# One pass over the gated outputs in the first output projection: both column halves of a chunk together

## The chip, the core and the metric

The kernel runs on one core of a Trainium2 chip. The metric is the device time of one execution in microseconds (us). The kernel before took 2925.76 us (median of 3 runs, 2924.88 to 2928.11). A profiled execution of its own took 2932.84 us, of which 2931.1 us lie between the first and the last instruction.

## The reference

The program is one inference step of a decoder with two layers, for a prompt of 2048 positions (width 1024) and a sample group of 8 sequences with 4 positions each. Layer A is gated linear attention with 4 heads of value width 512, layer B is sliding-window attention. Between them lies the part that matters here: layer A's gated output, 2048 wide, goes through an output projection and is added to the residual; the RMS-normalised sum then feeds the shared keys and values and layer B.

```python
o = rmsnorm(o, out_norm_g).reshape(bsz, seq_len, BRANCH_WIDTH)   # 2048 wide
d = (o * jax.nn.silu(gate)) @ w_out                               # 2048 x 1024
hp, hs = hp + dp, hs + ds
k_p, v_p = shared_kv(hp, kv_norm, w_k, w_v, k_norm, pos_p)        # normalises hp
q_p, g_p = swa_query(hp, b_norm[j], b_w_in[j], b_q_norm[j], pos_p)
```

The sample group has a recurrent state for each head and sequence (128 x 512 floats), which is read, used, updated and written back.

## The kernel before

The prompt is cut into 16 chunks of 128 positions and 4 blocks of four chunks. Every product is done in fp16 with operands split in a high and a low half, three matmuls for each product (`PASSES`), so a projection of one chunk on 512 output columns with 2048 inputs is 16 x 3 = 48 matmuls of 128x512.

Layer A runs over 4 heads and 4 blocks. For each chunk, `spill_og` (L613) writes the split gated output to a DRAM tensor, `ogd`. The output projection then reads it back transposed.

The **first output projection** (L1044 to L1050 and L1430 to L1435) goes over the chunks twice: a first pass makes columns 0 to 511 of all 16 chunks, a second pass columns 512 to 1023. `out_steps` (L981) of one chunk and half issues four transposing DMAs of 256 KB from `ogd` (`load`, L997) into four tiles (of the tags `sg` and `v` by turns, four buffers each), then the 48 matmuls into an accumulator `pj` (two buffers), then `a_finish` (L1015): load the input rows (`X`), add (VectorE, L1021), store to `hd`. In the second pass `a_finish` also loads the first half back from `hd` (`E`, L1025), and `norm_T` (L294) normalises the row, splits it and issues two more transposing DMAs (L315) that put it, transposed, into `uT`, the input of layer B.

Four SBUF tags matter. `W` has 12 slots of 4 KB for split weights; a unit of weights is 256 rows by 512 columns, so one half of the output weights takes 8 slots. `uT` has 4 slots of 16 KB; each holds the normalised inputs of one block, first of layer A, later of layer B. `wraw` (3 buffers) takes raw weights from DRAM, and `pst` (2 buffers) split weights on their way back to DRAM.

A **preparation step** (`prepare`, L236) is: load half a unit of raw weights of layer B (256 KB, SyncE queue, L219), round it on ScalarE (L193), take the remainder on VectorE (L194), both into a `pst` buffer, and store that to DRAM (256 KB, issued by GpSimd, L244). There are 104 such steps, and 8 small table steps. They are handed out by `some` between other work; layer B later fetches the prepared weights (`fetch`, L250, 512 KB).

The order of the work is that of program text as the framework's list scheduler rearranges it, fixed when the program is built: each engine and the SyncE queue work through their own list in order. An instruction at the head of a list that waits holds up all that is behind it on that engine. From layer B on (`pin`) the matmuls keep the order of the text.

The sample part of layer A (`SampleA.steps`, L674) has one step per sequence, `seq` (L762): it takes the state from a `W` slot (two sequences share one load of 512 KB), splits it, multiplies, updates it in place (L776) and stores it. For the last head these steps run beside the first output projection.

Of the kernel before, what the change touches and what calls it, by code (L numbers as in the profile page):

```python
# [9 lines left out]
F32 = mybir.dt.float32  # L10
# [9 lines left out]
P = 128  # L20
D = 1024
# [51 lines left out]
def _body(tc, nc, cp, sb, ps, dr, i, o):  # L73
# [67 lines left out]
    rtd = dr.tile([P, NCH, 4, HD], F32, tag="rtd", name="rtd")  # L141
    ogd = [dr.tile([P, 2, BW], F16, tag=f"ogd{c}", name=f"ogd{c}") for c in range(NCH)]
    ogd2 = [dr.tile([P, 2, BW], F16, tag=f"oge{c}", name=f"oge{c}") for c in range(NCH)]
    hd = [dr.tile([P, D], F32, tag=f"hd{c}", name=f"hd{c}") for c in range(NCH)]


# [144 lines left out]

        return [lambda part=todo[x : x + per]: step(part) for x in range(0, len(todo), per)], box

    def norm_T(xh, n, dst, both=False):  # L294
# [12 lines left out]
        for half in range(2):  # L307
            cs = slice(half * 512, half * 512 + 512)
            if both is None:
                pool.tensor_scalar(xh[half], xh[half], r[:n, 0:1], None, ALU.mult)  # L310
                split((xt[0][:n, cs], xt[1][:n, cs]), xh[half], eng=pool)
            else:
                split((xt[0][:n, cs], xt[1][:n, cs]), xh[half], r[:n, 0:1])
        for hl in range(2):
            nc.sync.dma_start(dst(hl), xt[hl][:n], transpose=True)  # L315

    uT = [T("uT", [P, KT, 2, 512], F16, 4) for _ in range(NBL)]
    uTs = C("uTs", [P, KT, 2, SMP], F16)
# [336 lines left out]
    class SampleA:  # L655
# [18 lines left out]
        def steps(self):  # L674
# [85 lines left out]
                mm(bx["po"], bx["Sh"], vst, start=True, stop=False)  # L760

            def seq(b):  # L762
                if b % 2 == 0:
                    bx["sr"] = T("W", [P, 2, 512], F32, NW)
                    nc.sync.dma_start(bx["sr"], i["state_gla"][0, b : b + 2, h].rearrange("b p v -> p b v"))
                sr = bx["sr"][:, b % 2]
                sh = T("pst", [P, 2, 512], F16, 2)
                split((sh[:, 0], sh[:, 1]), sr, SST)
                for n, (a, z) in enumerate(PASSES):
                    mm(bx["po"], bx["qm"][:, a, b, :], sh[:, z], start=False, stop=b == NS - 1 and n == 2)  # L770
                km = T("skn", [96, P], F16, 2)
# [5 lines left out]
                if b % 2:  # L777
# [91 lines left out]
    wo = out_w(i["a_w_out"][0], 0, gs_o)  # L869
# [6 lines left out]
    for n, (h, j) in enumerate(blocks):  # L876
# [23 lines left out]
        if last:  # L900
            ch = [cur.chunk_steps(c) for c in range(3)]
            weave([f for c in range(1, 4) for f in cur.vg_steps(c, (0,))], ch[0] + lv[:3] + ch[1][:3] + lv[3:5] + ch[2][:3])
            run(hw[h + 1].v.steps() if h + 1 < AH else wo.steps()[:8])
# [4 lines left out]
            run(hw[h + 1].g.steps() if h + 1 < AH else wo.steps()[8:])  # L908
        else:
            for c in range(3):  # L910
                more = side[c * 2 : c * 2 + 2] if n < 2 else some(PR[j])
# [69 lines left out]
    def out_steps(wo, half, ogs, finish, c):  # L981
        ot = []

        def load():
            if ogs is ogd2:
                t = T("uT", [P, 4, 8, P], F16, 4)
            elif half == 0 and c == 0:
                tt = [T("W", [P, 2, 8, P], F16, NW) for _ in range(2)]
                t = None
            for q in range(4):  # L990
                if ogs is ogd2:
                    ot.append(t[:, q])
                elif half == 0 and c == 0:
                    ot.append(tt[q // 2][:, q % 2])
                else:
                    ot.append(T(("sg", "v")[c % 2], [P, 8, P], F16, 4))
# [3 lines left out]
        return [load] + st + [lambda: finish(half, c, box[0])]  # L1000

    def out_sample(wo, half, finish_s):
        st, total = sproj_steps(wo.cols(4), 16, lambda: ogTs[0])
# [8 lines left out]

        return st + [fin]

    def a_finish(half, c, pp):  # L1015
        cs = slice(half * 512, half * 512 + 512)
        rows = slice(c * P, (c + 1) * P)
        xr = T("X", [P, 512], F32, 2)
        nc.sync.dma_start(xr, i["x_prompt"][0, rows, cs])
        h = T("st", [P, 512], F32, 2)  # L1020
        dve.scalar_tensor_tensor(h, pp, OSC, xr, ALU.mult, ALU.add)  # L1021
        nc.sync.dma_start(hd[c][:, cs], h)
        if half == 1:
            h0 = T("E", [P, 512], F32, 2)
            nc.sync.dma_start(h0, hd[c][:, :512])  # L1025
            cc = c % 4
            if cc == 0:
                uT[c // 4] = T("uT", [P, KT, 2, 512], F16, 4)
            u = uT[c // 4]
            norm_T((h0, h), P, lambda hl: u[:, :, hl, cc * P : (cc + 1) * P])  # L1030

    def a_finish_s(half, pt):
        cs = slice(half * 512, half * 512 + 512)
        xr = T("X", [SMP, 512], F32, 2)
# [6 lines left out]
            nc.sync.dma_start(h0, hsd[:, :512])  # L1041
            norm_T((h0, h), SMP, lambda hl: uTs[:, :, hl, :])

    weave(prev_tail, [f for c in range(7) for f in out_steps(wo, 0, ogd, a_finish, c)])  # L1044
    wo1 = out_w(i["a_w_out"][0], 1, gs_o)
    for c in range(7, NCH):
        weave(out_steps(wo, 0, ogd, a_finish, c), some() if c > 3 else [])
        if c == 12:
            run(out_sample(wo, 0, a_finish_s))
            run(wo1.steps())  # L1050


    def rope_mul(eng, t1, t2, src, ct, st):
# [373 lines left out]
            return [norm, square, norm_k, norm_q, split_q, norm_2, norm_3, cache, cache_2] + [lambda tq=tq, f=f: f(tq) for tq in range(2) for f in (att, att_2, att_3)]  # L1427


    for c in range(NCH):  # L1430
        weave(out_steps(wo1, 1, ogd, a_finish, c), some())
        if c == 8:
            run(gw[0].steps())
        if c == 10:
            run(out_sample(wo1, 1, a_finish_s))  # L1435

    pin[0] = True
    ORDER = "AffffffffBfAfffffffAfffAfBffff"
# [155 lines left out]
```

## Time and profile before

| | before |
|---|---|
| median of 3 runs | 2925.76 us |
| profiled execution | 2932.84 us |
| its span | 2931.1 us |
| TensorE (PE) busy | 2782.9 us, 95% |
| VectorE (DVE) busy | 1661.4 us, 57% |
| ScalarE (ACT) busy | 1387.7 us, 47% |
| GpSimd (POOL) busy | 1012.3 us, 35% |
| mean granted TensorE clock | 0.988 |

TensorE is the busy engine, so the questions are where it idles and who ends that idle time. The first output projection lies between 1154 and 1559 us of the span: first pass from 1154.2 to 1336.8, second pass from 1336.8 to 1559.2. Times in the views below are counted from the start of the span. "DMA share" is the mean busy share of the 16 DMA engines; it can go a little over 1, since packets overlap.

### The profile page before, as it was taken

The page shows a single profiled execution, that of the slowest core. Times are in us where ns is not written, and L with a number is a line of the kernel's source. Part 1 is how long each engine was busy: PE and PEld are TensorE (multiplying, and loading weights), DVE is VectorE, ACT ScalarE, POOL GpSimd, SP SyncE. Part 2 cuts the span into 40 slices and gives each one's busy share as a digit, 9 for nine tenths or more (in the row PEclk, how much of TensorE's full clock was granted, in tenths as well). Part 3 has the DMA queues.
Part 4 walks back from the last instruction along what each step waited for, and adds up shares of the span by engine and source line. Part 5 has one row for each costly group of instructions (what it writes and reads, how often), then busy time and mean ns, then how long its engine had stood idle before and what let it go on. Part 6 is the DMA issues. An engine that isn't in the chain of part 4 may idle for free.

```text
span 2931.1 us, 51443 instructions
## 1 busy us (share of the span) xinstructions
PE 2782.9 (95%) x19198; PEld 1400.0 (48%) x19198; DVE 1661.4 (57%) x3543; ACT 1387.7 (47%) x3289; POOL 1012.3 (35%) x1407
## 2 busy tenths in 40 slices
PE   6899999999999999999879999999999999999999
PEld 4445444544454444443334555555555555544444
DVE  6776777677767764222223666677767767730000
ACT  6655655465556554212232555566666566630000
POOL 2241233222212311001114676566566557520000
PEclk9999999999999999999999999999999999999999
DMA  8351243124212516999997566867857777799874
GB/s 216 78 131 37 83 133 114 35 90 157 85 55 90 187 37 149 193 237 252 241 227 185 106 127 122 200 111 129 176 112 132 154 145 139 146 225 173 176 148 98
DMA packets 881940, 412.75 MB, mean 141 GB/s; under 512 B 755344, under 2 KB 808536, under 8 KB 881656
## 3 DMA queue, kind: packets, MB, share of 16 engines
q1 hardware_dynamic: 870648, 380.02, 59.7%
q0 software_dynamic: 8960, 29.37, 2.7%
q8 instruction: 150, 2.46, 0.4%
q14 instruction: 102, 0.84, 0.1%
q10 hardware_dynamic: 2080, 0.07, 0.0%
HBM read 136.81 MB, written 99.16 MB: 81 GB/s over the span
## 4 chain that ended last, share of the span: by engine, by line
PE 56%; DMA 11%; DVE 10%; ACT 9%; issue 6%; POOL 5%; SPq 3%; ACTq 0%; DVEq 0%; POOLq 0%
PE pj L99 42%; PE tr L99 5%; PE o L99 4%; PE kv L99 3%; ACT o L1198 2%; DMA pre<-pst 2%; DMA pst<-v 2%; DVE v L194 1%; ACT v L193 1%; PE lev L99 1%; SPq L315 1%; DVE o L1193 1%; DMA wraw<-in_a_w_in_dram 1%; DMA uT<-ogT 1%; POOL ogT L191 1%
## 5 line engine op out<-in xcount | busy, mean ns | idle before, releaser
L99 PE MATMUL pj<-W,uT 128*128 128x512 f16 x6528 | 1514.1, 381 | 9.3 <-DVE sg L471 3.4
L99 PEld LDWEIGHTS <-uT 128*128 128x128 f16 x8064 | 775.2, 98 | 874.0 <-issue 40.0
L99 PE MATMUL tr<-W,uT 128*128 128x512 f16 x1536 | 365.7, 379 | 0.0
L1198 ACT ACTIVATE o<-o,mx 128x256 f32<-128x256 f32 (+1 forms) x384 | 168.6, 439 | 185.5 <-DVE mx L1193 175.9
L182 POOL TENSOR_SCALAR rs_m<-ss 128x1 f32<-128x1 f32 (+3 forms) x190 | 44.9, 236 | 607.0 <-ACT og L604 244.7
L99 PEld LDWEIGHTS <-X 128*128 128x128 f16 x2496 | 160.2, 98 | 123.1 <-issue 22.1
L191 POOL TENSOR_TENSOR ogT<-og,ogT 128x512 f16<-128x512 f32 x132 | 161.3, 1222 | 163.0 <-ACT ogT L190 158.6
L99 PE MATMUL pj<-uT,W 128*128 128x512 f16 (+1 forms) x912 | 186.8, 355 | 25.9 <-DMA uT<-ogT 22.6
L1193 DVE CUSTOM_DVE_ANT_0 o<-o,madd,nsink 128x256 f32<-128x256 f32 (+1 forms) x384 | 184.0, 479 | 44.6 <-PE o L99 39.6
L194 DVE SCALAR_TENSOR_TENSOR v<-o,v 128x512 f16<-128x512 f32 (+1 forms) x192 | 129.0, 672 | 117.5 <-ACT v L193 98.3
L99 PEld LDWEIGHTS <-W 128*128 128x128 f16 x2688 | 138.1, 98 | 118.6 <-issue 17.9
L99 PE MATMUL pj<-W,v 128*128 128x512 f16 x768 | 177.8, 388 | 16.8 <-DMA v<-ogd 16.7
L183 POOL TENSOR_TENSOR rs_r<-rs_m,mhalf 128x1 f32<-128x1 f32 (+2 forms) x186 | 185.4, 997 | 14.7
L244 POOL DMA_DIRECT2D pre<-pst x104 | 72.8, 701 | 338.1 <-DVE pst L194 326.7
L99 PE MATMUL pj<-W,sg 128*128 128x512 f16 x720 | 167.5, 389 | 16.5 <-DMA sg<-ogd 13.4
L1444 DVE SCALAR_TENSOR_TENSOR st<-pj,E 128x512 f32<-128x512 f32 x32 | 22.1, 692 | 269.7 <-PE pj L99 269.5
L501 POOL TENSOR_TENSOR E<-bt 128x256 f32<-128x256 f32 x96 | 73.7, 768 | 191.1 <-DVE X L191 111.4
L99 PEld LDWEIGHTS <-v 128*128 128x128 f16 x768 | 74.5, 100 | 115.5 <-DMA v<-ogd 26.3
L99 PE MATMUL o<-gl,X 128*128 128x256 f16 (+1 forms) x768 | 114.7, 273 | 10.6 <-DMA X<-qe 5.6
L642 ACT ACTIVATE ssg<-pj 128x64 f32<-128x64 f32 (+1 forms) x16 | 3.6, 242 | 253.2 <-PE pj L99 247.8
L99 PEld LDWEIGHTS <-sg 128*128 128x128 f16 x720 | 69.9, 100 | 110.5 <-DMA sg<-ogd 25.3
L99 PEld LDWEIGHTS <-sth 128*128 128x128 f16 x1984 | 100.9, 98 | 39.2 <-DMA sth<-v 10.5
(331 smaller groups left out, 4269.4 us busy)
## 6 DMA issues: line engine op xcount, KB each, us to landing
pre<-pst POOLq DMA_DIRECT2D x104, 256.0 KB, 4.0
W<-pre SPq DMA_DIRECT2D x52, 512.0 KB
ogd<-ogT SPq DMA_DIRECT2D x68, 256.0 KB
wraw<-in_a_w_in_dram SPq DMA_DIRECT2D x64, 256.0 KB
wraw<-in_b_w_in_dram SPq DMA_DIRECT2D x64, 256.0 KB
oge<-ogT SPq DMA_DIRECT2D x64, 256.0 KB
E<-hd SPq DMA_DIRECT2D x48, 256.0 KB
W<-in_state_gla_dram SPq DMA_DIRECT2D x16, 512.0 KB
```

Source lines behind the costliest of these rows:

```text
L99: return order(nc.tensor.matmul(*a, **k))
L182: pool.tensor_scalar(m[:n, :k], ss, a, b, ALU.mult, ALU.add)
L183: pool.tensor_tensor(r[:n, :k], m[:n, :k], mhalf[:n, :k], ALU.pow)
L191: eng.tensor_tensor(lo, src, hi, ALU.subtract)
L193: act(hi, src, AF.Copy, scale=sc)
L194: dve.scalar_tensor_tensor(lo, src, sc, hi, ALU.mult, ALU.subtract)
L244: nc.gpsimd.dma_start(self.pre[:, :, half * 512 : half * 512 + 512], t)
L315: nc.sync.dma_start(dst(hl), xt[hl][:n], transpose=True)
L501: pool.tensor_tensor(Ev[:, :, 0, :], ref, btv[:, :, 0, :], ALU.subtract)
L1193: dve.tensor_tensor_reduce(pm[:, z], pm[:, z], madd.rearrange("p a b -> p (a b)")[:, (2 - nk) * P :], -0.125, nsink[:, g * GRP + h : g * G ...
L1198: act(pm[:, z], pm[:, z], AF.Exp, scale=-1.0, bias=nm_[:, h : h + 1], accum_out=bx["sum"][:, h : h + 1])
L1444: dve.scalar_tensor_tensor(y, pp, OSC, hr, ALU.mult, ALU.add)
```

## The change

- Both halves of a chunk are made one after the other from one set of four transposed tiles (`a_out`). The gated outputs are read once: 64 transposing DMAs of 256 KB fewer.
- The first half of the sum stays in SBUF (tag `E`) until the second is there, so the 16 loads from `hd` go.
- Both halves of the weights must lie in SBUF at once: 16 units, 8 of the first half and 4 of the second in the 12 `W` slots, the other 4 in a `uT` slot whose inputs layer A has finished with (`wo_aside`). Another such slot takes the first chunk's transposed outputs. The second half's raw weights are now loaded in the last two blocks of layer A; in the last but one, 12 such loads with their conversions (8 of the second half, 4 of the first) stand where 6 preparation steps stood.
- Since two `uT` slots are taken, the last block's normalised inputs (chunks 12 to 15) go untransposed to DRAM (`ud`) and are brought back with 8 transposing DMAs at the end.
- The sample states of the last head no longer use `W` slots: each sequence has a load and a store of 256 KB of its own, in two buffers of tag `bt`.
- The preparation steps beside the projection are handed out five per chunk from chunk 4 on, where two stood per chunk and pass from chunk 7 of the first pass on.
- Layer B's first weights (`gw[0]`) are fetched where `W` slots come free: 8 units between the first and the second halves of chunks 14 and 15, 4 behind them, among the transposes from `ud`.

```diff
             def seq(b):
-                if b % 2 == 0:
-                    bx["sr"] = T("W", [P, 2, 512], F32, NW)
-                    nc.sync.dma_start(bx["sr"], i["state_gla"][0, b : b + 2, h].rearrange("b p v -> p b v"))
-                sr = bx["sr"][:, b % 2]
+                if h == AH - 1:
+                    sr = T("bt", [P, 512], F32, 2)
+                    nc.sync.dma_start(sr, i["state_gla"][0, b, h])
...
+    def wo_aside():
+        box_o["first"] = T("uT", [P, 4, 8, P], F16, 4)
+        t = T("uT", [P, 4, 2, 1024], F16, 4)
+        for u in range(4):
+            wo1.units[u].t = t[:, u]
...
+                if n == len(blocks) - 2:
+                    if c == 0:
+                        wo_aside()
+                    more = (wo1.steps()[:8] + wo.steps()[:4])[c * 4 : c * 4 + 4]
...
+    def a_out(c):
+        ot, hs = [], []
+        def load():
+            for q in range(4):
+                ot.append(box_o["first"][:, q] if c == 0 else T(("sg", "v")[c % 2], [P, 8, P], F16, 4))
+                nc.sync.dma_start(ot[q], ogd[c][:, q % 2, q // 2 * D : q // 2 * D + D], transpose=True)
+        def fin(half, pp):
+            xr = T("X", [P, 512], F32, 2)
+            nc.sync.dma_start(xr, i["x_prompt"][0, c * P : (c + 1) * P, cs])
+            h = T(("E", "st")[half], [P, 512], F32, 2)
+            dve.scalar_tensor_tensor(h, pp, OSC, xr, ALU.mult, ALU.add)
+            nc.sync.dma_start(hd[c][:, cs], h)
+            hs.append(h)
+            if half == 0:
+                return
+            if c >= NCH - 4:
+                norm_T(hs, P, lambda hl: ud[cc][:, hl], flat=True)
+                return
...
-    weave(prev_tail, [f for c in range(7) for f in out_steps(wo, 0, ogd, a_finish, c)])
-    wo1 = out_w(i["a_w_out"][0], 1, gs_o)
-    for c in range(7, NCH):
-        weave(out_steps(wo, 0, ogd, a_finish, c), some() if c > 3 else [])
+    for c in range(lead):
+        todo += [aout[c + 1][0]] + aout[c][1][0] + aout[c][1][1]
+    weave(prev_tail, todo)
+    for c in range(lead, tail):
+        aout[c + 1][0]()
+        weave(aout[c][1][0] + aout[c][1][1], some(5))
...
-    for c in range(NCH):
-        weave(out_steps(wo1, 1, ogd, a_finish, c), some())
-        if c == 8:
-            run(gw[0].steps())
+    aout[NCH - 1][0]()
+    weave(aout[tail][1][0] + aout[tail + 1][1][0], some(99))
+    run(gw[0].kv[0].steps() + gw[0].q.steps())
+    weave(aout[tail][1][1] + aout[tail + 1][1][1], [])
+    run(gw[0].g.steps())
+    uT[NBL - 1] = T("uT", [P, KT, 2, 512], F16, 4)
+    for c in range(4):
+        for hl in range(2):
+            nc.sync.dma_start(uT[NBL - 1][:, :, hl, c * P : (c + 1) * P], ud[c][:, hl], transpose=True)
```

Two places of the fixed order, as built. The first is VectorE in the changed kernel, from the end of chunk 4's first half (`E<-pj,X`) to the end of chunk 5's first half; `pst<-wraw` is VectorE's part of a preparation step, `ogT` that of the normalisation.

```order
L1031 SCALAR_TENSOR_TENSOR E_13545<-pj_13482,X_13543 128x512
L195 SCALAR_TENSOR_TENSOR pst_13671<-wraw_13672,gsb,pst_13671 128x512
L195 SCALAR_TENSOR_TENSOR pst_13697<-wraw_13698,gsb,pst_13697 128x512
L195 SCALAR_TENSOR_TENSOR pst_13725<-wraw_13726,gsb,pst_13725 128x512
L195 SCALAR_TENSOR_TENSOR pst_13751<-wraw_13752,gsb,pst_13751 128x512
L195 SCALAR_TENSOR_TENSOR pst_13795<-wraw_13796,gsb,pst_13795 128x512
L1031 SCALAR_TENSOR_TENSOR st_13611<-pj_13548,X_13609 128x512
L195 SCALAR_TENSOR_TENSOR pst_13834<-wraw_13835,gsb,pst_13834 128x512
```

The same engine in the kernel before, in the second pass, from the end of one chunk's half (`st<-pj,X`) past the next.

```order
L1021 SCALAR_TENSOR_TENSOR st_14861<-pj_14804,X_14859 128x512
L304 TENSOR_TENSOR ss_14867<-ss_14867 128x1
L194 SCALAR_TENSOR_TENSOR ogT_14876<-E_14864,rs_r_14872,ogT_14875 128x512
L194 SCALAR_TENSOR_TENSOR ogT_14876<-st_14861,rs_r_14872,ogT_14875 128x512
L194 SCALAR_TENSOR_TENSOR pst_14697<-wraw_14698,pst_14697 128x512
L194 SCALAR_TENSOR_TENSOR pst_14736<-wraw_14737,pst_14736 128x512
L1021 SCALAR_TENSOR_TENSOR st_14954<-pj_14897,X_14952 128x512
```

Between two finished halves there were two preparation steps; in the changed kernel there are 5, then 4, 4, 3, 5, 3, 5, 6, 4, 4 and 1 up to the end of chunk 9, so 43 stand between the end of chunk 4's first half and that of chunk 9's.

The second place is the SyncE queue where the last head's states go through, in the changed kernel, from the first state's store on (`bt`; `sg<-ogd` are the transposed outputs of chunk 4).

```order
L786 DMA out_st_s_dram<-bt_13085 128x512
L769 DMA bt_13164<-in_state_gla_dram 128x512
L786 DMA out_st_s_dram<-bt_13124 128x512
L769 DMA bt_13200<-in_state_gla_dram 128x512
L1032 DMA hd_135<-E_13161 128x512
L1029 DMA X_13367<-in_x_prompt_dram 128x512
L786 DMA out_st_s_dram<-bt_13164 128x512
L1024 DMA_TRANSPOSE sg_13280<-ogd_101 128x8x128
L769 DMA bt_13239<-in_state_gla_dram 128x512
L1024 DMA_TRANSPOSE sg_13282<-ogd_101 128x8x128
```

And in the kernel before, where the four loads of that head's states stand together.

```order
L616 DMA ogd_112<-ogT_12761 256x1x512
L765 DMA W_12988<-in_state_gla_dram 128x2x512
L765 DMA W_13061<-in_state_gla_dram 128x2x512
L765 DMA W_13138<-in_state_gla_dram 128x2x512
L765 DMA W_13205<-in_state_gla_dram 128x2x512
L1022 DMA hd_129<-st_12721 128x512
```

A load of the third state and of each later one now stands in the queue behind the store of the state whose buffer it takes.

## Rows read from the trace of the kernel before

**Rows 1.** The page: busy time by engine, and PE in 40 slices.
```profile
PE 2782.9 (95%) x19198; PEld 1400.0 (48%) x19198; DVE 1661.4 (57%) x3543; ACT 1387.7 (47%) x3289; POOL 1012.3 (35%) x1407
...
PE   6899999999999999999879999999999999999999
```
**Rows 2.** Stages: length, busy us (count) by engine, clock, DMA share, GB/s.
```profile
1000.00:1030.00 30.00, 25.04 (x163) 11.87 (x162) 28.12 (x50) 19.75 (x36) 13.80 (x19) 1.00 0.64 205
...
1154.20:1336.80 182.60, 180.57 (x950) 81.76 (x949) 47.46 (x95) 37.98 (x67) 12.51 (x20) 1.00 1.00 217
1336.80:1559.20 222.40, 186.90 (x902) 79.16 (x900) 58.23 (x100) 62.99 (x129) 34.89 (x63) 0.94 1.09 243
1559.20:1600.00 40.80, 39.53 (x188) 17.85 (x187) 11.77 (x25) 10.93 (x28) 21.28 (x30) 1.00 0.67 189
```
**Rows 3.** PE in order of time: start, length, operation, count, idle before.
```profile
1336.69 10.52 PE L99 MATMUL pj<-W,sg 128*128 128x512 f16 x48
1347.05 10.52 PE L99 MATMUL pj<-W,v 128*128 128x512 f16 x48
...
1359.71 5.35 PE L99 MATMUL pj<-W,sg 128*128 128x512 f16 x24 [1.71 <-DMA sg<-ogd]
```
**Rows 4.** What PE waited for, 1080 to 1620 us: total, times, longest.
```profile
PE pj L99 <- DMA v<-ogd: 16.7, 17, 2.7
PE pj L99 <- DMA sg<-ogd: 13.4, 13, 2.5
...
PE pj L99 <- DVE st L1021: 3.1, 1, 3.1
```
**Rows 5.** SyncE's queue in order of time, second pass.
```profile
1356.45 0.88 SPq L219 DMA_DIRECT2D wraw<-in_b_w_out_dram  x2
1357.42 1.23 SPq L997 DMA_TRANSPOSE sg<-ogd  x1
1358.75 0.53 SPq L1022 DMA_DIRECT2D hd<-st  x1
1359.37 2.59 SPq L997 DMA_TRANSPOSE sg<-ogd  x1
```
**Rows 6.** DMA packets, 1336.8 to 1559.2 us.
```profile
DMA packets 107372, 54.00 MB, mean 243 GB/s; under 512 B 94812, under 2 KB 94812, under 8 KB 107359
```
**Rows 7.** Stores of preparation steps (L244), 980 to 1024 us: starts, landing.
```profile
L244 POOL DMA_DIRECT2D pre<-pst x15: 678/684/730, 982.2 to 1022.8; - x15
...
DMA to landing us min/median/max: 3.0/3.5/4.1
```
**Rows 8.** The same stores, 1236 to 1272 us.
```profile
L244 POOL DMA_DIRECT2D pre<-pst x11: 688/690/690, 1236.5 to 1271.0; - x11
...
DMA to landing us min/median/max: 3.6/5.5/6.1
```
**Rows 9.** The same stores, 1336.8 to 1559.2 us.
```profile
DMA to landing us min/median/max: 3.3/4.8/6.5
```
**Rows 10.** Groups, 1154 to 1337 us: busy, mean ns, idle before and releaser.
```profile
L194 DVE SCALAR_TENSOR_TENSOR pst<-wraw,gsb,pst 128x512 f16<-128x512 f32 x11 | 8.2, 749 | 26.9 <-ACT pst L193 26.9
L193 ACT ACTIVATE pst<-wraw,gsb 128x512 f16<-128x512 f32 x11 | 7.8, 718 | 29.0 <-DMA pre<-pst 29.0
...
L99 PE MATMUL pj<-ogTs,W 128*128 128x64 f16 (+1 forms) x128 | 3.6, 183 | 0.0
```
**Rows 11.** PE and VectorE at one state step in order of time.
```profile
1195.32 0.39 PE L99 MATMUL kv<-ke,skn 96*128 96x512 f16 x1
...
1200.72 0.38 PE L99 MATMUL kv<-ke,skn 96*128 96x512 f16 x1
```
**Rows 12.** VectorE there.
```profile
1201.14 0.69 DVE L776 SCALAR_TENSOR_TENSOR W<-kv,W 128x512 f32<-128x512 f32 x1 [1.13 <-PE kv L99]
```
**Rows 13.** Chain of waits: a raw-weight load from issue to its reader.
```profile
1112.64 2.81 DMA wraw<-in_a_w_out_dram
...
1356.45 4.79 DMA wraw<-in_b_w_out_dram
```

More of the change, by code (lines that the diff above doesn't have):

```diff
@@ L143, in _body @@
     ogd2 = [dr.tile([P, 2, BW], F16, tag=f"oge{c}", name=f"oge{c}") for c in range(NCH)]
+    ud = [dr.tile([P, 2, D], F16, tag=f"ud{c}", name=f"ud{c}") for c in range(NCH - 4, NCH)]
     hd = [dr.tile([P, D], F32, tag=f"hd{c}", name=f"hd{c}") for c in range(NCH)]
@@ L314, in norm_T @@
         for hl in range(2):
-            nc.sync.dma_start(dst(hl), xt[hl][:n], transpose=True)
+            if flat:
+                nc.sync.dma_start(dst(hl), xt[hl][:n])
+            else:
+                nc.sync.dma_start(dst(hl), xt[hl][:n], transpose=True)
     uT = [T("uT", [P, KT, 2, 512], F16, 4) for _ in range(NBL)]
@@ L762, in seq @@
             def seq(b):
-                if b % 2 == 0:
-                    bx["sr"] = T("W", [P, 2, 512], F32, NW)
-                    nc.sync.dma_start(bx["sr"], i["state_gla"][0, b : b + 2, h].rearrange("b p v -> p b v"))
-                sr = bx["sr"][:, b % 2]
+                if h == AH - 1:
+                    sr = T("bt", [P, 512], F32, 2)
+                    nc.sync.dma_start(sr, i["state_gla"][0, b, h])
+                else:
+                    if b % 2 == 0:
+                        bx["sr"] = T("W", [P, 2, 512], F32, NW)
+                        nc.sync.dma_start(bx["sr"], i["state_gla"][0, b : b + 2, h].rearrange("b p v -> p b v"))
+                    sr = bx["sr"][:, b % 2]
                 sh = T("pst", [P, 2, 512], F16, 2)
@@ L868, in _body @@
     run(hw[0].g.steps())
-    wo = out_w(i["a_w_out"][0], 0, gs_o)
+    wo, wo1 = (out_w(i["a_w_out"][0], half, gs_o) for half in range(2))
+    box_o = {}
+    def wo_aside():
[3 more added lines that the diff above has]
+            wo1.units[u].t = t[:, u]
     blocks = [(h, j) for h in range(AH) for j in range(NBL)]
@@ L902, in _body @@
             weave([f for c in range(1, 4) for f in cur.vg_steps(c, (0,))], ch[0] + lv[:3] + ch[1][:3] + lv[3:5] + ch[2][:3])
-            run(hw[h + 1].v.steps() if h + 1 < AH else wo.steps()[:8])
+            run(hw[h + 1].v.steps() if h + 1 < AH else wo.steps()[4:])
             for c in range(1, 4):
@@ L907, in _body @@
                 f()
-            run(hw[h + 1].g.steps() if h + 1 < AH else wo.steps()[8:])
+            run(hw[h + 1].g.steps() if h + 1 < AH else wo1.steps()[8:])
         else:
             for c in range(3):
-                more = side[c * 2 : c * 2 + 2] if n < 2 else some(PR[j])
+                if n == len(blocks) - 2:
+                    if c == 0:
+                        wo_aside()
+                    more = (wo1.steps()[:8] + wo.steps()[:4])[c * 4 : c * 4 + 4]
+                else:
+                    more = side[c * 2 : c * 2 + 2] if n < 2 else some(PR[j])
                 weave(cur.vg_steps(c + 1, (0, 1) if n else (1,)), mix(cur.chunk_steps(c) + lv[(0,3,6)[c]:(3,6,8)[c]], sparts[(0,3,7)[c]:(3,7,99)[c]]) + more)
@@ L984, in load @@
         def load():
[L985 to L989, printed above, removed]
-            for q in range(4):
[L991 to L996, printed above, removed]
+            t = T("uT", [P, 4, 8, P], F16, 4)
+            for q in range(4):
+                ot.append(t[:, q])
                 nc.sync.dma_start(ot[q], ogs[c][:, q % 2, q // 2 * D : q // 2 * D + D], transpose=True)
@@ L1000, in out_steps @@
         return [load] + st + [lambda: finish(half, c, box[0])]
+    def a_out(c):
[5 more added lines that the diff above has]
+        def fin(half, pp):
+            cs = slice(half * 512, half * 512 + 512)
+            xr = T("X", [P, 512], F32, 2)
[6 more added lines that the diff above has]
+                return
+            cc = c % 4
+            if c >= NCH - 4:
+                norm_T(hs, P, lambda hl: ud[cc][:, hl], flat=True)
+                return
+            if cc == 0:
+                uT[c // 4] = T("uT", [P, KT, 2, 512], F16, 4)
+            u = uT[c // 4]
+            norm_T(hs, P, lambda hl: u[:, :, hl, cc * P : (cc + 1) * P])
+        out = []
+        for half, w in enumerate((wo, wo1)):
+            st, box = proj_steps(lambda: PT("pj", [P, 512], bufs=2), lambda k, a: ot[k // 8 * 2 + a][:, k % 8, :], w, 16)
+            out.append(st + [lambda half=half, box=box: fin(half, box[0])])
+        return load, out
     def out_sample(wo, half, finish_s):
@@ L1013, in out_sample @@
         return st + [fin]
[L1015 to L1030, printed above, removed]
     def a_finish_s(half, pt):
@@ L1042, in a_finish_s @@
             norm_T((h0, h), SMP, lambda hl: uTs[:, :, hl, :])
-    weave(prev_tail, [f for c in range(7) for f in out_steps(wo, 0, ogd, a_finish, c)])
-    wo1 = out_w(i["a_w_out"][0], 1, gs_o)
-    for c in range(7, NCH):
-        weave(out_steps(wo, 0, ogd, a_finish, c), some() if c > 3 else [])
-        if c == 12:
-            run(out_sample(wo, 0, a_finish_s))
-            run(wo1.steps())
+    aout = [a_out(c) for c in range(NCH)]
+    tail = NCH - 2
+    lead = 4
+    aout[0][0]()
+    todo = []
+    for c in range(lead):
[4 more added lines that the diff above has]
+        weave(aout[c][1][0] + aout[c][1][1], some(5))
+        if c == 7:
+            for half, w in enumerate((wo, wo1)):
+                run(out_sample(w, half, a_finish_s))
     def rope_mul(eng, t1, t2, src, ct, st):
```

8 lines of the change are left out of this document (4 added, 4 removed).

## The prediction

> **What bounds the kernel now.** The page comes first: TensorE is busy for 95% of the span, and of the 40 slices only two in the middle (1392 to 1539 us) show 8 and 7 tenths; the first two belong to the start [rows 1]. So something is to be had where the projection's second pass runs, or nowhere much. The view by stages gives the size: in the first pass TensorE works 180.57 of 182.6 us, in the second 186.90 of 222.4 us, with a mean granted clock of 0.94, and the DMA share is 1.00 and 1.09 [rows 2]. Next the order in time on TensorE: two halves of 48 matmuls that nothing holds up start 1336.69 and 1347.05 us, 10.36 us apart; after the second, the next half begins in pieces, each behind a transposing DMA [rows 3]. The waits say the same for the stage: 16.7 and 13.4 us for transposed outputs, 3.1 us for VectorE [rows 4]. Each of these waits is short, but there are 30 of them.
>
> Why the transposes are late: they stand in SyncE's queue, which never rests there, and a transposing DMA costs the queue 1.23 us when it finds room and 2.59 us when it does not, against 0.4 to 0.5 us for a plain one [rows 5]. The 16 DMA engines are full. In the second pass 94,812 of 107,372 packets are short ones, and these belong to 96 transposes (4 of `ogd` and 2 of `uT` for each chunk), about 990 each [rows 6]. A transpose moves 256 KB, so the 96 move 25 of the 54.0 MB. Where plain DMAs dominate, a share of 0.64 carries 205 GB/s, 320 GB/s at a full share [rows 2]; the other 29 MB are then 90 us of all engines, and of 1.09 x 222.4 = 242 us the transposes take 152: 1.6 us each, where a plain 256 KB takes 0.8. That is why half the transposes matter.
>
> What the second pass would take if nothing held it up: 16 x 10.36 = 165.8 us, and 3.6 us for the sample's small matmuls [rows 3, 10]. It takes 222.4. **53 us are lost** there, slow clock included, and 2 us in the first pass: 55 us.
>
> **The change part by part.** *Second pass merged into the first.* A chunk now has 20.7 us of matmuls, and besides preparation the DMA engines get 6 transposes and 4 plain 256 KB for it (two `X`, two `hd`): 9.6 + 3.3 = 12.9 us. Before, the second pass asked for 9.6 + 5 x 0.8 and two stores of preparation, 15 us, in 10.36 us. The four transposes of the next chunk have a chunk, 20.7 us, to land, where they had a half. So the waits for `v<-ogd` and `sg<-ogd` go, and the loads of `E<-hd` with them. Removed: 55 us, if nothing else is late. Three things are.
>
> *Preparation steps.* In the built order 43 of them stand on VectorE between the end of chunk 4's first half and the end of chunk 9's. TensorE's work in that stretch is 10 halves, 103.6 us, and the sample's two small products (2 x 3.6 us and their transposes, together 8 us): 112 us. The accumulator has two buffers, so TensorE may run one half, 10.4 us, ahead of VectorE. If a step takes p, TensorE waits 43 x p - 122 us in all. What is p? A step needs one of two `pst` buffers and keeps it for ScalarE's 0.72, VectorE's 0.75 us [rows 10] and the store's landing. At a landing of 5.5 us two buffers give (1.45 + 5.5) / 2 = 3.5 us; measured are 10 intervals in 34.5 us, 3.45 us, with ScalarE waiting 29.0 us for `pre<-pst` [rows 8, 10]. In layer A, with a landing of 3.5 us, 14 intervals take 40.6 us: 2.90 us [rows 7]. These are the two ends. The DMA share was 0.64 around the one [rows 2] and about 1 at the other (the first pass has 1.00). In the changed kernel 8.8 steps a chunk at p = 3.3 us are 29 us, in which DMAs ask for 12.9 + 8.8 x 1.6 = 27 us, a share of 0.93; that is nearer to the second, and I take p = 3.3: **20 us** of waiting (3 at 2.90, 26 at 3.45). It shows as TensorE waiting for VectorE's L1031, not for a DMA.
>
> The Trainium skill (DMA: Bandwidth & Descriptors, section "Anatomy of one DMA") fits such a DMA as 2.0 us plus bytes over 436 GB/s, an estimate of 2.6 us for these 256 KB. By it p would be 2.0 us and the term nothing. The trace disagrees: the shortest landing is 3.0 us, the median in the second pass 4.8 us [rows 7, 9].
>
> *States of the last head.* A sequence's `kv` matmul comes every 5.4 us [rows 11]. State b+2 now needs the buffer of state b: from `kv` to `kv` of two later, VectorE 0.69 us [rows 12], a store, its landing, a load, its landing, then the split of about 1.4 us. A 256 KB load took 2.81 us from issue to reader in a quiet stretch, 4.79 us in a full one [rows 13], and a 256 KB store lands in 3.5 to 5.5 us [rows 7, 8]. With 3.5 us for each the ring takes 0.7 + 7 + 1.4 + two issues at 0.5, near 10 us, against 10.8 us of TensorE's work; but SyncE's queue stands still while it waits for the store, and transposes at 1.2 to 2.6 us stand between [rows 5]. Three turns of the ring, each late by 0 to 5 us: 0 to 15 us, I take **5**. The price is bounded, not read, since no ring of this kind runs before.
>
> *Weights.* In the last but one block 12 conversions replace 6 steps, 4.5 us more on a VectorE that is busy 28.12 of 30 us where TensorE already idles 5 us [rows 2]. It may cost 0 to 5 us or nothing beyond the idle time; I take **2**. The late second-half weights are needed only 15 us into chunk 0, which hides them.
>
> *The end.* Eight fetches go out while chunk 15's first half frees the slots, 20.7 us before they are read; the last four in the last 5 us, and the gate weights are read 10.4 us into layer B. Layer B starts with an idle time of 1.3 us now [rows 2]. The 8 added transposes are 13 us of DMA time at a place with a share of 0.67. I take **1** (between -1 and 4). The two `ud` stores a chunk replace two transposes and are cheaper; with room on the DMA engines there, nothing.
>
> The sum: 55 - 20 - 5 - 2 - 1 = 27 us less. The profiled execution, 2932.84 us, would be 2906; the median shown lies 7.1 us below that execution, and from 2925.8 us the same step gives **2899 us**.
>
> **The rivals.** *Full recovery* (chance 0.20): the steps run at layer A's 2.90 us and the ring is hidden. Then 3 + 1 of the 55 us stay, 2875 us. For it: only the packets that are gone make DMA room; against it, the share of 0.93 that the steps themselves bring. The fit of the Trainium skill named above would lead here too; the rows speak against its 2.6 us.
>
> *The wait changes hands* (0.14): steps at 3.45 us and a ring late by 15 us: 26 + 15 us, and 5 for weights and end: 46 us return, 2917 us, and up to no change where the landing reaches the 6.5 us that was seen once in the second pass [rows 9]: p = 4.0, 50 us.
>
> *Slower* (0.08): the same chain of preparation, beyond that point. All 43 steps sit in front of finished halves on VectorE, so a landing of 7.0 us, p = 4.2, costs 59 us, and with the other 8 us the time is 2938 us. It decides from a landing of 6.7 us on. For it: the order crowds 8.8 steps into a chunk, where two in 10.36 us already came with landings of 5.5 us. Against it: a stalled TensorE issues fewer transposes, which shortens the landing.
>
> *That the change does not do what it says* is not open: the built order has 64 transposes of `ogd` instead of 128.
>
> **How the numbers follow.** Forecast 0.58 (2884 to 2913 us), full recovery 0.20 (2866 to 2884), the wait changes hands 0.14 (2913 to 2932), slower 0.08. A measurement can tell 0.2%, about 6 us, from no change. The range from 2870 to 2921 us holds the forecast, most of full recovery and a part of the third case. Faster by more than 0.2% (below 2920): 0.58 + 0.20 + 0.06 = 0.84; within: 0.08; slower: 0.08.
>
> **What would show it.** Right: in the stage TensorE's waits for `v<-ogd` and `sg<-ogd` are below 5 us together; a wait for VectorE's L1031 stands first, between chunks 4 and 9; chunks 10 to 15 run at 20.7 us each with a DMA share well under 1; stores of preparation come every 3.2 to 3.4 us; the clock stays near 1. Wrong: TensorE still waits for transposes, or waits at `o<-pst` in the state steps for more than 15 us, or layer B begins with more than 5 us of waiting for `W<-pre`.

## The result, and the profile after

The changed kernel takes **2900.35 us** (median of 4 runs, 2895.21 to 2904.33) against 2926.94 us for the kernel before on the same chip (4 runs, 2924.88 to 2938.87). The ratio, taken from the mean times, is 0.99, with a 95% interval from 0.9869 to 0.9931: faster by 0.7 to 1.3%. The forecast was 2899 us.

The profiled execution has a span of 2898.0 us, 33.1 us less than that of before. The page after, in the lines of [rows 1] (busy time of the engines, TensorE in 40 slices) and two lines more: the granted clock in tenths, and the packets of the whole span.
```profile
PE 2769.2 (96%) x19198; PEld 1401.8 (48%) x19198; DVE 1661.5 (57%) x3543; ACT 1386.7 (48%) x3289; POOL 1012.0 (35%) x1407
...
PE   6899999999999999997999999999899999999999
...
PEclk9999999999999999998999999999999999999999
...
DMA packets 813331, 393.86 MB, mean 136 GB/s; under 512 B 687760, under 2 KB 740952, under 8 KB 813048
```
The two weak slices of the second pass have become one, at 1304 to 1377 us. The matmuls are as many as before (19,198). Of the packets under 512 B 67,584 are gone (755,344 before), 1056 for each of the 64 transposes that the change drops, near the 990 worked out from [rows 6].

What such a transpose costs can be read from the page's line on the DMAs that SyncE issues (packets, MB, share of the 16 engines' span), before and after:
```profile
q1 hardware_dynamic: 870648, 380.02, 59.7%
q1 hardware_dynamic: 802040, 361.14, 56.3%
```
59.7% of 2931.1 us less 56.3% of 2898.0 us are 118 us of all engines. The 18.9 MB that went are the 64 transposes and, net, 8 plain DMAs of 256 KB (16 reloads fewer, 8 stores to `ud` more). With the plain ones at the prediction's 0.8 us that leaves an estimated 1.7 to 1.8 us for a transpose.

The stages after, in the columns of [rows 2]; the first row begins at chunk 0, the last but one ends with chunk 15.
```profile
1153.40:1184.00 30.60, 30.60 (x144) 13.87 (x142) 10.67 (x31) 12.69 (x27) 4.02 (x7) 1.00 0.76 172
1184.00:1247.00 63.00, 63.00 (x289) 25.86 (x288) 21.02 (x42) 17.75 (x35) 3.13 (x8) 1.00 0.72 157
1247.00:1289.00 42.00, 41.76 (x194) 18.82 (x194) 15.38 (x25) 14.09 (x24) 10.14 (x17) 1.00 1.03 263
1289.00:1338.80 49.80, 43.31 (x193) 19.14 (x193) 16.03 (x25) 15.02 (x27) 12.41 (x20) 0.97 0.97 263
1338.80:1361.40 22.60, 8.66 (x245) 8.39 (x245) 7.14 (x12) 7.02 (x14) 6.31 (x10) 0.70 0.89 236
1361.40:1400.00 38.60, 38.60 (x200) 17.94 (x197) 13.78 (x23) 12.87 (x25) 9.24 (x16) 1.00 1.00 268
1400.00:1528.20 128.20, 128.20 (x595) 58.10 (x594) 19.30 (x33) 17.92 (x39) 5.81 (x14) 1.00 0.71 161
1528.20:1570.00 41.80, 41.80 (x202) 19.27 (x201) 13.40 (x31) 11.41 (x30) 24.74 (x36) 1.00 0.69 165
```
The second number is the length, the third TensorE's busy time: outside 1289 to 1361 us TensorE rests for 0.24 us in all. The projection took 405.0 us (1154.20 to 1559.17) and takes 374.8 (1153.35 to 1528.17): **30.2 of the 33.1 us** are here, 0.85 us ahead of it, 2.1 us behind it. Of chunks 10 and 11 the first halves start (columns as in [rows 3]):
```profile
1403.68 10.52 PE L99 MATMUL pj<-W,sg 128*128 128x512 f16 x48
...
1424.40 10.52 PE L99 MATMUL pj<-W,v 128*128 128x512 f16 x48
```
What is left of waiting, in the columns of [rows 4], 1060 to 1600 us:
```profile
PE pj L99 <- DVE st L1031: 18.1, 3, 12.9
PE pj L99 <- DVE E L1031: 1.6, 2, 1.3
PE tr L102 <- DVE ssg L647: 1.0, 1, 1.0
PE pj L99 <- DVE ssg L647: 0.5, 1, 0.5
```
Not one wait for a transpose remains, where [rows 4] have 30.1 us. The 19.7 us for L1031 are five waits, all for finishes of chunks 5 to 7. The longest of them, on VectorE in order of time (columns as in [rows 12]):
```profile
1338.05 0.68 DVE L1031 SCALAR_TENSOR_TENSOR E<-pj,X 128x512 f32<-128x512 f32 x1
1340.93 0.69 DVE L195 SCALAR_TENSOR_TENSOR pst<-wraw,pst 128x512 f16<-128x512 f32 x1 [2.20 <-ACT pst L194]
1344.71 0.69 DVE L195 SCALAR_TENSOR_TENSOR pst<-wraw,pst 128x512 f16<-128x512 f32 x1 [3.08 <-ACT pst L194]
1346.31 0.69 DVE L195 SCALAR_TENSOR_TENSOR pst<-wraw,pst 128x512 f16<-128x512 f32 x1 [0.91 <-ACT pst L194]
1350.36 0.69 DVE L195 SCALAR_TENSOR_TENSOR pst<-wraw,pst 128x512 f16<-128x512 f32 x1 [3.36 <-ACT pst L194]
1354.00 0.69 DVE L195 SCALAR_TENSOR_TENSOR pst<-wraw,pst 128x512 f16<-128x512 f32 x1 [2.95 <-ACT pst L194]
1354.61 0.69 DVE L1031 SCALAR_TENSOR_TENSOR st<-pj,X 128x512 f32<-128x512 f32 x1
```
VectorE works 0.69 us of every 3.3 us and waits for ScalarE the rest. Five steps stand in its order between two finishes; the second finish, whose product was complete on TensorE, comes 16.6 us after the first. The steps' stores and what waits for a landing, 1235 to 1400 us (count and starts; landing minimum, median, maximum):
```profile
L245 POOL DMA_DIRECT2D pre<-pst x47: 686/687/732, 1243.4 to 1398.2; - x47
...
  ACT pst L194: 76.1, 30
...
DMA to landing us min/median/max: 2.7/4.5/7.0
```
46 intervals in 154.8 us are 3.37 us a step; ScalarE waits 76.1 us for landed stores. Between the end of chunk 4's first half (1259.83 us) and that of chunk 9's (1400.17 us) the 43 steps take 140.3 us, 3.26 us each. In the kernel before, in the stretch of [rows 7], what waited for a landing there was:
```profile
  ACT pst L193: 7.5, 4
```

### The profile page after: what moved, and what is told of

Its sections match the earlier page's. It is cut to its first block, busy times and chain, and to the rows that moved or that the text cites. A ratio compares the mean times of both kernels' runs of the same rounds, so it can differ in the third digit from the quotient of the medians.

```text
span 2898.0 us, 51309 instructions
## 1 busy us (share of the span) xinstructions
PE 2769.2 (96%) x19198; PEld 1401.8 (48%) x19198; DVE 1661.5 (57%) x3543; ACT 1386.7 (48%) x3289; POOL 1012.0 (35%) x1407
## 3 DMA queue, kind: packets, MB, share of 16 engines
q1 hardware_dynamic: 802040, 361.14, 56.3%
## 4 chain that ended last, share of the span: by engine, by line
PE 59%; DVE 10%; ACT 9%; DMA 9%; issue 7%; POOL 5%; SPq 1%; POOLq 0%; ACTq 0%; DVEq 0%
PE pj L99 45%; PE tr L99 6%; PE o L99 4%; PE kv L99 3%; DMA pre<-pst 2%; ACT o L1237 2%; DMA wraw<-in_a_w_in_dram 2%; DVE v L195 1%; DMA pst<-v 1%; ACT v L194 1%; PE lev L99 1%; DVE o L1232 1%; POOL pre L245 1%; DVE W L195 1%; DVE lev L1232 1%
## 5 line engine op out<-in xcount | busy, mean ns | idle before, releaser
L99 PEld LDWEIGHTS <-uT 128*128 128x128 f16 x8224 | 788.1, 98 | 892.6 <-issue 49.3
L99 PEld LDWEIGHTS <-X 128*128 128x128 f16 x2496 | 159.9, 98 | 120.9 <-issue 20.7
L99 PE MATMUL pj<-W,v 128*128 128x512 f16 x576 | 128.3, 379 | 0.0
L194 ACT ACTIVATE v<-o 128x512 f16<-128x512 f32 (+1 forms) x192 | 111.3, 580 | 7.4 <-DMA sth<-v 3.7
L191 ACT ACTIVATE ogT<-og 128x512 f16<-128x512 f32 x132 | 82.2, 623 | 64.7 <-DVE og L611 44.2
```

What stands on the lines that cost most here:

```text
L99: return order(nc.tensor.matmul(*a, **k))
L191: act(hi, src, AF.Copy)
L194: act(hi, src, AF.Copy, scale=sc)
```

## The experiments

The theory has two halves. **T1**: the second pass was slow because the 16 DMA engines were full, and what filled them were the transposes. **T2**: the 20 us that are left come from preparation steps which stand on VectorE in front of finished halves, more of them than TensorE's work covers at their pace. The rivals are named with each run. All times are medians; ratios are of mean times, to the kernel before on the same chip. Where a run has a time "finish to finish", it is that from the first finished half to the last, in its one profiled execution: 361.7 us in the changed kernel (1166.5 to 1528.2) and 361.5 us when it was run again.

**Half the transposes of `ogd` in the second pass, two passes kept** (x1, made from the kernel before; it leaves out the low parts of the outputs there and takes the tiles of the high parts in their place).
```
             for q in range(4):
+                if ogs is ogd and half == 1 and q % 2:
+                    ot.append(ot[q - 1])
+                    continue
```


> The kernel before, with one edit: in the second pass each half fetches only the two transposed tiles of the high parts, and uses them for the low parts too (the low parts of ogd are left out of the second column half). Theory, the 16 DMA engines are full of transposes: 32 of 96 transposes of the second pass go, 1.6 us of all engines each, so a half there asks for 12 us of DMA time instead of 15; the second pass shrinks from 222 us by about 35 to 45 us, time 2882 to 2892 us against 2927. Rival, the second pass is held by VectorE, by the reload of hd or by order alone: the transposes that go were waited for by nobody in particular, less than 10 us, 2917 to 2927 us.

Measured: 2892.75 us, ratio 0.9871 (0.9853 to 0.989), 37 us less than the 2930.17 of before: inside T1's 35 to 45 us, and 0.75 us above its range of times, which was counted from 2927. TensorE's waits from 1330 to 1620 us, and the first half of the second pass, in the kernel before and here:
```profile
PE pj L99 <- DVE st L1024: 9.0, 4, 4.6
PE tr L102 <- DVE ssg L643: 2.7, 1, 2.7
```
```profile
1336.00:1440.00 104.00, 89.83 (x384) 37.29 (x383) 28.73 (x48) 30.85 (x61) 16.38 (x29) 0.95 1.12 257
1336.00:1440.00 104.00, 98.56 (x445) 43.98 (x444) 36.43 (x61) 37.45 (x74) 21.99 (x38) 0.97 1.10 289
```
Half of one sort of DMA removed, all waits for it gone, though the engines are about as full at first (1.10) as before (1.12): they now carry 289 GB/s instead of 257. So the transposes were what TensorE waited for, and the rival falls. Whether they cost by filling the engines or by holding SyncE's queue, this run can't tell, since each transpose left out also leaves the queue. It keeps two passes and gains about what the change gains, and 9 us of waiting for VectorE appear at once where transposes were waited for.

**Plain DMAs off SyncE's queue** (x2, made from the kernel before). SyncE's queue shows no rest in the stretch of [rows 5]; it might have been the limit rather than the engines behind it.
```
+        q = nc.gpsimd if half == 1 else nc.sync
-        nc.sync.dma_start(xr, ...)
+        q.dma_start(xr, ...)
...
```
The store of `h` and the reload of `h0` take `q` in the same way.

> The kernel before, with one edit: in the second pass the three plain DMAs of a half (load of X, store of hd, reload of hd) are issued by GpSimd's queue instead of SyncE's. Bytes and descriptors stay the same. Theory, the DMA engines are full: no change beyond 8 us, 2919 to 2935 us, the second pass still near 222 us. Rival, SyncE's issue time is the limit (6 transposes and 5 plain DMAs a half, one after the other, stores waiting at the head of the queue): 3 x 0.45 us and the waits for VectorE leave the queue in each of 16 halves, 22 us or more, below 2905 us.

Measured: 2948.64 us, ratio 1.0056 (1.0035 to 1.0076): slower, by 18 us on the medians. Both expectations missed, T1's by 14 us, the rival's by 44 us and in sign. TensorE waits more for the same transposes, 43.9 us instead of 30.1 (1330 to 1620 us), and the stores of preparation land later (1336 to 1550 us: KB each, median us to landing; 4.9 in the same stretch of before):
```profile
PE pj L99 <- DMA sg<-ogd: 24.6, 12, 4.1
PE pj L99 <- DMA v<-ogd: 19.3, 11, 3.8
```
```profile
pre<-pst POOLq DMA_DIRECT2D x30, 256.0 KB, 6.5
```
A queue relieved of three of its about eleven DMAs in each half delivered its transposes no sooner. That speaks against the queue as the limit, but the run isn't a clean test of it. What waited in its trace, and in that of before for SyncE's queue (both 1340 to 1550 us):
```profile
POOL E L1026 <- DVE ogT L194: 101.6, 12, 14.3
...
SPq L997 <- PE pj L99: 23.0, 16, 3.8
```
The first line is x2: the reloads of `E` now stand at the head of GpSimd's own list until VectorE has freed their buffer, 101.6 us in all, with the stores of preparation and the norm's steps on GpSimd behind them. How much of the 18 us comes from that stays open. The second line says more on the rival: before the change SyncE's queue did rest, 23.0 us, at transposes whose tile TensorE was still reading, while the share of the engines was 1.12, 1.09 and 1.05 in the pass's three stretches (1336 to 1440, to 1510, to 1560 us). That fits full engines better than a full queue. Whether more tile buffers, and so earlier transposes, would have helped was not run.

**The transposes put back into the changed kernel** (a5): one pass, but each half fetches its own four tiles.
```
-    ... T(("sg", "v")[c % 2], [P, 8, P], F16, 4))
+    ... T(("sg", "v")[half], [P, 8, P], F16, 4))
-    out.append(st + [lambda half=half, box=box: fin(half, box[0])])
+    out.append((st if half else [lambda: load(1)] + st) + [...])
```


> The changed kernel, with one edit: each column half of a chunk fetches its own four transposed tiles, so that the number of transposes is again that of before, while one pass, the kept h, the weights' place and the order of the preparation stay. Theory, the halved transposes are what the change gains by: 10 transposes and 4 plain DMAs a chunk ask for 19.3 us beside 20.7 us of matmuls, and with 8.8 preparation stores and loads at 1.6 us in the chunks of the steps for 33 us; six such chunks are late by 12 us each, and waits for v<-ogd and sg<-ogd come back: 25 to 60 us, 2925 to 2960 us. Rival, the gain came from h that is kept instead of reloaded and from one pass over the chunks: less than 10 us, 2900 to 2910 us.

Measured: 2924.6 us, ratio 0.9981 (0.9969 to 0.9992), 24 us above the changed kernel's 2900.35. That is 0.4 us below the foot of what T1 expected, and far above the rival. TensorE's waits, 1060 to 1600 us, and the stage from 1400 us on:
```profile
PE pj L99 <- DMA sg<-ogd: 13.0, 6, 5.1
PE pj L99 <- DVE st L1033: 12.1, 2, 10.7
...
PE pj L99 <- DMA v<-ogd: 4.4, 5, 1.9
```
```profile
1400.00:1550.00 150.00, 143.18 (x650) 63.02 (x649) 28.47 (x47) 27.30 (x55) 14.23 (x27) 0.99 1.07 239
```
The waits for transposes are back, 17.4 us, and the share from 1400 us on is 1.07, where the changed kernel has 0.71. With x1 this shows from both sides that the number of transposes costs the time. The return is smaller than I had it in the middle of the range, and the edit moved one thing more than the expectation says: the built order of the steps did not stay. In a5 35 of them stand between the first halves of chunks 4 and 9, where the changed kernel has 43, and the rest stand behind, up to chunk 10. So 12.1 us of waiting for VectorE, where the changed kernel has 18.1, are not those of the same order, and the 24 us are not the price of the transposes alone.

**h kept or reloaded** (a7): the first half's h goes out and comes back, as before.
```
-            h = T(("E", "st")[half], [P, 512], F32, 2)
+            h = T("st", [P, 512], F32, 2)
...
+            h0 = T("E", [P, 512], F32, 2)
+            nc.sync.dma_start(h0, hd[c][:, :512])
```


> The changed kernel, with one edit: the first half's h is stored and loaded again for the norm, as before the change, instead of being kept. Transposes, order of the halves and the weights' place stay. Theory, the transposes are the gain: 16 plain loads more are 16 x 0.8 = 13 us of the DMA engines, beside waits of about 20 us that are VectorE's; 0 to 8 us, 2900 to 2908 us. Rival, the kept h is a part of the gain of its own, since a reload behind a store makes the norm and what stands behind it on VectorE late: 10 to 25 us, 2910 to 2925 us.

The changed kernel was run once more beside it:

> The changed kernel once more, on the same chip as the two experiments beside it, as their measure: 2900 us, 2895 to 2905.

Measured: a7 2901.97 us, ratio 0.9929 (0.9907 to 0.995), where the theory had it; the changed kernel 2890.51 us (2885.21 to 2900.6), 0.9895 (0.987 to 0.992), 4.5 us below its expected 2895 to 2905. By medians that is 11 us, though the intervals overlap. The stage doesn't show them: TensorE waits 15.6 us for L1031 in a7 and 18.0 in the changed kernel, and from the first finished half to the last the trace has 360.5 and 361.5 us. Of the 6.9 us between the two spans 3.3 lie ahead of the stage and 4.6 in layer B, while the changed kernel's own two profiled spans are 10.7 us apart. So the reload costs nothing that the stage's rows show; a cost of a few us in the total is neither shown nor excluded.

**The steps spread out** (a2): VectorE's part of a step stands in order behind the last finished half. The work is the same.
```
-            dve.scalar_tensor_tensor(h, pp, OSC, xr, ALU.mult, ALU.add)
+            gate[0] = dve.scalar_tensor_tensor(h, pp, OSC, xr, ALU.mult, ALU.add).ins
-                split((dst(0), dst(1)), raw, SW)
+                after_gate(split((dst(0), dst(1)), raw, SW))
```
`after_gate` adds a dependency that counts for the order alone, without a semaphore. Between finished halves VectorE's order then has 2 or 3 steps from chunk 4 to chunk 13 and one more in front of chunk 14's first half, where the changed kernel has 3, 5, 4, 4, 3, 5, 3, 5, 6, 4, 4 from chunk 4's first half to chunk 9's first, then one, then none.

> The changed kernel, with one edit: VectorE's part of a preparation step stands in order behind the last finished half, so that 2 or 3 steps stand between two halves on VectorE, from chunk 4 to chunk 14, instead of 43 between chunk 4 and chunk 9. The work is the same. Theory, 43 steps at 3.3 us in front of the finished halves are what the remaining 20 us of waiting come from: 2.4 steps at 3.3 us are 8 us beside 10.4 us of matmuls, nothing is late, and 15 to 22 us go: 2878 to 2885 us. Rival, the DMA engines behind the steps are the limit and the wait only moves (to transposes, to the weights of layer B): less than 6 us, 2894 to 2904 us.

Measured: **2877.19 us**, ratio 0.9817 (0.9801 to 0.9832) where the changed kernel has 0.99 and 0.9895: the fastest of all, 23 and 13 us below its two medians, and 0.8 us below T2's range. Finish to finish it takes 339.8 us (1167.0 to 1506.8), 21.9 us less than the changed kernel. TensorE's waits from 1060 to 1600 us, all of them, and the stages of the stall:
```profile
PE pj L99 <- DVE ssg L653: 0.8, 1, 0.8
PE pj L99 <- issue: 0.6, 1, 0.6
PE o L99 <- ACT pst L194: 0.5, 1, 0.5
```
```profile
1289.00:1338.80 49.80, 49.22 (x412) 25.54 (x411) 15.21 (x25) 13.66 (x27) 10.57 (x18) 1.00 1.09 247
1338.80:1361.40 22.60, 22.50 (x155) 10.99 (x151) 6.92 (x12) 7.22 (x15) 2.90 (x5) 1.00 0.68 178
...
1400.00:1528.20 128.20, 128.20 (x596) 58.08 (x595) 30.52 (x52) 28.75 (x58) 25.22 (x41) 1.00 0.92 233
```
The steps still wait for landings (median 5.4 us, 4.5 in the changed kernel), and TensorE no longer waits for them. The DMA share of chunks 10 to 15 rises from 0.71 to 0.92: the room that was idle there is what the spread uses. T2 holds as to place and size.

**More buffers for the steps** (a6): steps take turns between `pst` and `qe`, an idle pair of the same size.
```
+                turn[0] += 1
+                tag = ("pst", "qe")[turn[0] % 2] if wide[0] else "pst"
-                t = T("pst", [P, 2, 512], F16, 2)
+                t = T(tag, [P, 2, 512], F16, 2)
```


> The changed kernel, with one edit: the preparation steps of the stage take turns between pst and another pair of buffers of the same size that is idle there, four buffers instead of two. The order on VectorE stays crowded, 43 steps between the first half of chunk 4 and the end of chunk 9. Theory, a step takes p because its buffer waits for the store to land, and TensorE waits 43 p - 122 us: with four buffers p falls to the loads' pace, (4.8 + 1.45) / 3 = 2.1 us by three wraw buffers, or to what a DMA share of 1 allows, 2.6 us; both are below the 2.84 us at which the sum is zero, so 15 to 20 us go: 2880 to 2886 us. Rival, the DMA engines set the pace of the steps, not the buffers: p stays at 3.2 to 3.4 us, the idle time of ScalarE changes from pre<-pst to wraw loads, less than 6 us, 2895 to 2904 us.

Measured: 2895.36 us, ratio 0.991 (0.9891 to 0.9929): no gain that can be told from the changed kernel, as the rival had it, and 360.2 us finish to finish. But the rival's reason failed too: the steps did come faster, 22 stores of one buffer pair from 1253.0 to 1373.9 us, 2.88 us a step. What had moved was the order: with four buffers 43 steps stood in front of 9 finished halves in a row instead of 10 (the next expectation says two halves less; it is one). Pace and crowding had changed together. One half less takes 10.4 us from the 122 us of cover: 43 x 2.88 - 112 is 12 us, and TensorE waited 13.9 us for L1035. (The 2.6 us that the expectation gives for a DMA share of 1 is worked out from no row.)

**The same four buffers, in the changed kernel's order** (a10): as a6, and each step held behind the finished half that it stands behind in the changed kernel, so that the counts per half are those listed above.
```
+    counts = [0, 0, 0, 0, 0, 0, 0, 2, 3, 5, 4, 4, 3, 5, 3, 5, 6, 4, 4, 1]
+    behind_half = [n - 1 for n, x in enumerate(counts) for _ in range(x)]
...
+                    gate[0] = done[behind_half[turn[0]]]
```


> The changed kernel with four buffers for the preparation steps, as in the run before, but with as many steps between each two finished halves on VectorE as the changed kernel itself has, since four buffers alone also packed 43 steps into two halves less. There the steps came every 2.88 us (22 of one kind, two intervals of 2.88 us in 5.76). Theory, the pace of the steps times their number is what TensorE waits for: 43 x 2.88 - 122 = 2 us, TensorE waits for VectorE's L1044 for less than 7 us, and 12 to 18 us go from the stage: 2880 to 2888 us. Rival, DMA engines at a share of 1 set the pace whatever the buffers: steps every 3.2 to 3.4 us, 14 us of waiting or more, 2890 to 2902 us as the changed kernel.

Measured: 2886.56 us, ratio 0.9864 (0.9845 to 0.9882), an interval that overlaps those of the changed kernel; finish to finish the trace has 348.9 us (1163.0 to 1511.9), 12.8 us less. TensorE's waits, 1060 to 1600 us, and ScalarE's longest for DMAs, 1247 to 1400 us:
```profile
PE pj L99 <- DVE st L1044: 6.5, 1, 6.5
PE tr L102 <- DVE ssg L660: 2.3, 1, 2.3
```
```profile
ACT qe L194 <- DMA wraw<-in_b_w_out_dram: 31.6, 10, 5.6
...
ACT pst L194 <- DMA wraw<-in_b_w_out_dram: 21.8, 7, 6.5
```
48 intervals from 1235.77 to 1383.83 us are 3.08 us a step, against 3.32 in the changed kernel counted in the same way, and the wait for L1044 is 6.5 us, where the changed kernel waits 19.7 and 18.0 us for L1031 in its two profiles. The time lies in the theory's 2880 to 2888 us, the pace between the theory's 2.88 and the rival's 3.2 us. So the buffers did hold the steps back, but they give 0.24 us a step and no more: ScalarE now waits for raw weights, which have three buffers, where it waited for landed stores. By the prediction's formula 43 x 3.08 - 122 would be 10 us, 4 more than measured. Whether the loads' buffers or the engines (a share of 1.09 from 1247 to 1339 us) set 3.08 was not separated.

## Why the prediction was right

- **Removed, 55 us.** Right. The waits for `v<-ogd` and `sg<-ogd` were to be below 5 us together; they are 0. Chunks 10 to 15 were to take 20.7 us each with a share well under 1; the first halves of chunks 10 and 11 start 20.72 us apart, at a share of 0.71. x1 and a5 show that the transposes made the waits; that they did so by filling the engines rests on the shares and on the rests of SyncE's queue. The prediction's sentence that this queue never rests there was wrong (23.0 us of rest, shown at x2). Its price of 1.6 us a transpose was about right: the pages give 1.7 to 1.8.
- **Preparation steps, 20 us.** Right in place and size: 19.7 us of waiting for L1031, all of it for the finishes of chunks 5 to 7, none beyond. The pace was taken as 3.3 us and is 3.26 to 3.37, by the stretch that one counts; 43 x 3.26 - 122 is 18 us, 43 x 3.32 - 122 is 21 us. a2 shows the cause, a10 that the pace counts. How the pace comes about is less well hit. With the measured landing of 4.5 us the prediction's formula for two buffers gives (1.45 + 4.5) / 2 = 2.98 us and 6 us of waiting. The 3.3 us was chosen between two measured paces, and the lower one, layer A's 2.90 us, was not set by the buffers: in the stretch of [rows 7] ScalarE waited for landed stores only 4 times in 15 steps. So the size owes something to luck. What makes up the other 0.3 to 0.4 us of a step was not resolved.
- **Ring of states, 5 us.** Wrong by 5, inside its 0 to 15: from 1184 to 1247 us TensorE works 63.00 of 63.00 us. ScalarE did wait for the loads of the states, 25.5 us for six of them, but TensorE had matmuls of the projection to go on with. The share there is 0.72; in a5, where it is 0.96 from 1153 to 1247 us, TensorE does wait, 4.4 us at `o<-pst`. The prediction had counted landings of 3.5 us and let the 5 us stand for a queue that stands still; what lateness there was reached ScalarE and not TensorE.
- **Weights, 2 us, and the end, 1 us.** Both came out just below nothing: 0.85 us gained ahead of the stage, and 2.1 behind it, where the idle 1.3 us at layer B's start are gone. That is no more than two executions differ by.
- **The sum.** By terms the profiled execution should have lost 27 us and lost 33.1. In the projection 55 us were to go and 25 to come back (20 and 5); it is 30.2 us shorter, so about 25 did come back, but not in those two terms. The ring gave nothing, and the stall cost nearer 24 than 20: beside the 19.7 us for L1031, 1.5 us of waiting at the sample's small steps and nearly 3 us of matmuls at a lower granted clock (last section), which the prediction did not have. The 6 us of difference are the small terms, 3 us lost on paper and 3 gained. That the median hit to 1.4 us owes something to chance, since the changed kernel's medians on two occasions were 2900.35 and 2890.51 us.
- **The rivals.** Full recovery had 2875 us; a2 comes to 2877.19 us, not by a faster pace of the steps (2.90 us) as that case had it, but by their order. "The wait changes hands" was partly so: 30.1 us for transposes became 19.7 us for VectorE. The slower case needed landings of 6.7 us; the median was 4.5, the maximum 7.0.

## What to carry to other kernels

Where DMA engines are full, count the work that each kind of DMA gives them, not its bytes: here a transpose took, by the estimate above, about twice what a plain DMA of as many bytes does, and leaving out 32 of them gave 37 us. When such a wait goes, look at what the order puts in front of the next release: slow steps that were harmless between long waits cost 20 us in front of finished halves, and tying them to the pace of the halves brought it back without taking away any work. An experiment that changes buffers or transfers can also change a built order, as a5 and a6 did; hold the order fixed, as in a10, or two effects mix unseen.

## What the runs showed of the hardware

Spreading DMAs over a second queue did not help full engines: with 39 plain DMAs of 256 KB on GpSimd's queue (14, 13 and 12 from 1336 to 1550 us) the preparation stores landed in 6.5 us instead of 4.9, and the kernel became 0.56% slower; GpSimd's own waits, named at x2, are a part of that run.

And a wait for VectorE cost TensorE more than its length. Two stretches behind such waits, with the granted clock as the third number from the end, and what ran there:
```profile
1302.70:1309.30 6.60, 6.59 (x25) 2.71 (x25) 2.89 (x5) 3.19 (x6) 2.99 (x5) 0.79 1.03 257
1355.30:1359.80 4.50, 4.42 (x107) 4.29 (x106) 2.14 (x4) 3.26 (x7) 2.35 (x4) 0.50 0.83 190
```
```profile
1302.71 6.72 PE L99 MATMUL pj<-uT,sg 128*128 128x512 f16 x24 [3.15 <-DVE st L1031]
...
1355.35 0.80 PE L99 MATMUL pj<-ogTs,uT 128*128 128x64 f16 x16 [12.92 <-DVE st L1031]
1355.96 0.83 PE L99 MATMUL pj<-ogTs,W 128*128 128x32 f16 x16
1356.60 0.83 PE L99 MATMUL pj<-ogTs,uT 128*128 128x64 f16 x16
```
Behind 12.92 us of idling the clock is at the lower of its two levels, 0.50 (1.2 of 2.4 GHz), and the sample's groups of 16 matmuls start 0.64 us apart. In the spread kernel, where TensorE's longest rest among them is 0.58 us, such groups start 0.44 us apart. That is 0.2 us for each of nearly seven groups, 1.3 us. Behind 3.15 us of idling, at a mean of 0.79, 24 matmuls take 6.72 us, where [rows 3] have 5.35: 1.4 us more.
